# A decoder step on one core: the order in which attention, feed-forward and the samples' work are emitted

## The chip, the cores and the metric

One NeuronCore of a Trainium2 chip runs the whole step in one launch. The metric is the device time of that launch in microseconds (us). The kernel is written with a tile framework: the program emits instructions, and a scheduler at build time places them on the five engine queues (TensorE = PE, VectorE = DVE, ScalarE = ACT, GpSimd = POOL, SyncE = SP, which issues every DMA here). Each queue then runs strictly in the order in which it was written.

## The reference

One layer of a hybrid decoder is run for a prompt (1 sequence of 2048 tokens) and for 8 samples (1 new token each, 1024 tokens of paged past), all in fp32, with D = 1024 and a feed-forward width of 2816.

```python
h = rmsnorm(x) * (1 + sc1) + sh1                      # modulated by c
qkv, z, beta, a, aq, ak, av, iq, ik, iw = split(h @ w_in)
# group 1: gated DeltaNet, 4 heads of 128
#   prompt: chunks of 64; sample: one recurrent step on a 128x128 state per head
s = s * exp(g);  delta = (v - k @ s) * beta;  s = s + outer(k, delta);  o = q @ s
# group 2: sparse attention, 4 heads, 2 kv heads
score = sum_h iw[h] * relu(iq[h] @ ik.T)              # 8 index heads of 64
idx = top_k(score, 256); o_att = softmax(q @ k[idx]) @ v[idx]
x = x + ga1 * (concat(o_gdn, o_att) @ w_out)
x = x + ga2 * ((silu(gate) * up) @ w_ffn_out)         # gate, up = h2 @ w_ffn_in
y = rmsnorm(x)
```

For the prompt the keys of a query are those at or before it, for a sample its 1024 past keys and the new one (1025). New keys, values, convolution rows and recurrent states are outputs too.

## The kernel before, in words

**Precision.** A wide product is done as three fp32r matmuls (`mm3`, lines 157 to 159): both operands are split into a high part and a remainder. `weights` (lines 130 to 146) loads a 128x512 weight tile by DMA (line 140), casts the high part on ACT (line 141) and forms the remainder on DVE (line 142); there are three such tiles (`wi`) and two raw ones (`wr`). For the samples, `mm_s` adds two matmuls per weight tile (lines 173, 174).

**Phase 1** (to about 1430 us) projects the four groups of 512 tokens and runs the DeltaNet chunks; it leaves its results in DRAM. Attention of blocks 0 to 3 (128 queries each) is done there as well.

**Phase 2** has its own pool of buffers. `groups` (lines 1179 to 1190) emits, for g = 0 to 3: the attention of the next four blocks, `ffn(g)`, and after `ffn(0)` the copy of the samples' cache pages (`copy_pages`, 192 copies issued by SP). `sample_steps` is emitted after the attention of blocks 12 to 15 and ahead of `ffn(2)`. What is emitted earlier has the higher priority in the scheduler: where two instructions are ready for an engine, it takes the one emitted first, and a later one fills what is left. An instruction whose buffer is not free can't be placed.

**Attention of a block** is `index` (scores of 8 heads on PE, relu on ACT line 1238, weighted sum on DVE line 1245), then `select` (lines 1119 to 1154), then `attend` (lines 1263 to 1313), which ends with the store of `oT`, of which there is one buffer. `select` looks for the 256th largest score by ten halvings of a threshold: each counts on DVE the scores above it (line 1139) and moves it (lines 1140, 1141); a second part takes out up to 16 keys that are left over. The number of keys still missing is kept in `far`; if any row ever misses more than 16, all of phase 2 is run again with the exact form (`groups(True)`, lines 1174 to 1177).

**`ffn(g)`** multiplies by w_out, adds to x, normalizes, multiplies by w_ffn_in, forms the gated product and multiplies by w_ffn_out. `ffn(3)` carries the 8 samples with it: their output of both head groups (`oTs`) is an operand of its first weight tiles, so its first weight tile is not done before the samples' attention is. Per group it has 192 + 1056 + 528 = 1776 matmuls of `mm3`; `ffn(3)` has 296 of `mm_s` more.

**`sample_steps`** (lines 987 to 1109): the scores of 1025 keys for 8 samples (lines 1027 to 1043), the exact choice of 256 keys by `topk` (32 times line 1116, the 8 largest, and line 1117, which takes them out), then `sample_gdn`, then scores, softmax and values over the whole past with a bias for the keys not chosen (lines 1057 to 1102). It uses attention's buffers: `sc`, `oT`, `PT`, `big`, `qT`, `iqT`, and the PSUM buffers `g` and `s` (two each).

**`sample_gdn`** (lines 881 to 984): the recurrent step. Its small tiles are two `rl` buffers and its large ones the two `big` buffers of attention; the states come in two loads of 1 MB (four samples each).

Of the kernel before, what the change touches and what calls it, by code (L numbers as in the profile page):

```python
# [33 lines left out]
T = 2048  # L34
NS = 8
# [5 lines left out]
H = 4  # L41
# [12 lines left out]
KR = 3  # L54
# [53 lines left out]
class K:  # L108
# [772 lines left out]
    def sample_gdn(self):  # L881
        nc, p, A, O = self.nc, self.p2, self.A, self.O
        raws = self.raws

        def P():
            return self.ps.tile([128, 512], F32, name="g", tag="g", bufs=2)

        def small(*shapes):

            tl, o, views = p.tile([128, 512], F32, name="rl", tag="rl", bufs=2), 0, []  # L890
            for sh in shapes:
                n = int(np.prod(sh))
                v = tl[:, o:o + n]
                views.append(v if len(sh) == 1 else v.rearrange("p (a b) -> p a b", b=sh[1]))
                o += n
            return views

        def big():
            return p.tile([128, T], F32, name="big", tag="big", bufs=2)

        stT, a, b = small((12, 24), (12, NS), (12, NS))
        y, sq, dg, btf, de, o, s2 = small((12, NS), (64,), (64,), (64,), (H, NS), (32,), (32,))
        st, nq = big()[:24, 0:1536], big()[:NS, 0:1536]
        nc.sync.dma_start(st, A["state_conv"][0].rearrange("n i c -> (n i) c"))
        nc.sync.dma_start(O[10][0, :, 0:2, :], A["state_conv"][0, :, 1:3, :])
        pt = P()
        for m in range(12):
            nc.tensor.transpose(pt[:, m * 24:(m + 1) * 24], st[:, m * 128:(m + 1) * 128], self.id[:24, :24])
        nc.vector.tensor_copy(stT, pt[:, :288].rearrange("p (m x) -> p m x", m=12))
        for c in range(3):  # L910
            pt = P()
            for m in range(4):
                nc.tensor.transpose(pt[:NS, m * 128:(m + 1) * 128], raws[:, c * 4 + m, :], self.id)
            nc.vector.tensor_copy(nq[:, c * 512:(c + 1) * 512], pt[:NS])
        nc.sync.dma_start(O[10][0, :, 2, :], nq)
# [28 lines left out]

        for x in range(2):
            S = big().rearrange("p (b h e) -> p b h e", h=H, e=128)
            sl = slice(x * 4, x * 4 + 4)
            nc.sync.dma_start(S, A["state_ssm"][0, sl].rearrange("n h d e -> d n h e"))
            pk = P()
            for s in range(4):  # L950
                for h in range(H):
                    nc.tensor.matmul(pk[:, h * 4 + s:h * 4 + s + 1], S[:, s, h, :], y[:, 4 + h, x * 4 + s:x * 4 + s + 1], start=True, stop=True)
            d = de[:, :, sl]
            nc.vector.tensor_tensor(d, pk[:, :16].rearrange("p (h n) -> p h n", h=H), bt[:, 1, :, sl], op=OP.mult)
            nc.vector.tensor_tensor(d, y[:, 8:12, sl], d, op=OP.subtract)
            nc.vector.tensor_tensor(d, d, bt[:, 0, :, sl], op=OP.mult)
            for s in range(4):
                n = x * 4 + s
                nc.gpsimd.tensor_tensor(S[:, s], S[:, s], bt[:, 1, :, n].unsqueeze(2).to_broadcast([128, H, 128]), op=OP.mult)
                pd = P()  # L960
                for h in range(H):
                    nc.tensor.transpose(pd[:, h * 128:(h + 1) * 128], de[:, h, n:n + 1].to_broadcast([128, 128]), self.id)
                for h in range(H):
                    nc.vector.scalar_tensor_tensor(S[:, s, h, :], pd[:, h * 128:(h + 1) * 128], y[:, 4 + h, n:n + 1], S[:, s, h, :],
                                                   op0=OP.mult, op1=OP.add)
            nc.sync.dma_start(O[11][0, sl].rearrange("n h d e -> d n h e"), S)
            po = P()
            for s in range(4):
                for h in range(H):
                    nc.tensor.matmul(po[:, h * 4 + s:h * 4 + s + 1], S[:, s, h, :], y[:, h, x * 4 + s:x * 4 + s + 1], start=True, stop=True)  # L970
            nc.vector.tensor_copy(o.rearrange("p (h n) -> p h n", h=H)[:, :, sl], po[:, :16].rearrange("p (h n) -> p h n", h=H))
# [7 lines left out]
        gz = big()[:NS, :512]  # L979
# [7 lines left out]
    def sample_steps(self):  # L987
# [16 lines left out]
        b = q.tile([128, T + 16], F32, name="sc", tag="sc", bufs=2)  # L1004
        wk, pr = b[:NS, 0:NK], b[:32, NK:2 * NK]
# [113 lines left out]
    def select(self, pool, w, bias, sums, i):  # L1119


        nc = self.nc
        n = (i + 1) * 128
        s, c = w[:, :n], bias[:, :n]
        v = pool.tile([128, 24], F32, name="sv", tag="sv", bufs=2)
        W = pool.tile([128, SEARCH], F32, name="sW", tag="sW", bufs=2)
# [9 lines left out]
        nc.vector.tensor_scalar(W, self.pw, rg, None, op0=OP.mult)  # L1136
# [8 lines left out]
        nc.vector.scalar_tensor_tensor(self.far[:, 0:1], d, -16.0, self.far[:, 0:1], op0=OP.add, op1=OP.max)  # L1145
        nc.vector.scalar_tensor_tensor(self.far[:, 1:2], d, -1.0, self.far[:, 1:2], op0=OP.mult, op1=OP.max)
        nc.vector.scalar_tensor_tensor(s, c, -(2.0 ** 116), s, op0=OP.mult, op1=OP.add)
        nc.gpsimd.memset(w[:, n:n + 16], PAD)
        for a in range(2):
            nc.vector.max(m8, s)  # L1150
            nc.vector.tensor_scalar(a8, self.io[:, a * 8:a * 8 + 8], d, 3.0e38, op0=OP.is_lt, op1=OP.mult)
            nc.vector.scalar_tensor_tensor(m8, a8, PAD, m8, op0=OP.add, op1=OP.min)
            nc.vector.match_replace(w[:, :n + 16], m8, w[:, :n + 16], GONE)
        nc.vector.tensor_scalar(c, s, -1.0e34, NEG, op0=OP.is_ge, op1=OP.mult)
# [36 lines left out]

    def buffers(self):

        p = self.p2
        one = lambda tag, w, bufs=1, dt=F32: lambda: p.tile([128, w], dt, name=tag, tag=tag, bufs=bufs)
        return dict(pool=p, kT=one("kT", 512, KR), V=one("V", 512, KR), ikT=self.ikT, qT=one("qT", 512), iqT=one("iqT", 1024), sc=one("sc", T + 16, 2),
                    bias=one("bias", T, 2, BF), big=one("big", T, 2), rl=one("rl", 512, 2),
                    PT=one("PT", 512, 2), oT=one("oT", 512, OB))
# [24 lines left out]
    def index(self, i, B, general):  # L1223
        nc, p = self.nc, B["pool"]
        n = (i + 1) * 128
        if i >= 2:
# [24 lines left out]
            else:  # L1251
                self.select(p, sc, bias, None if sums is None else sums[:, :len(self.widths(n))], i)
# [83 lines left out]
    def ffn(self, g):  # L1336
# [27 lines left out]
        if samp:  # L1364
            xrows = q.tile([128, T + 16], F32, name="sc", tag="sc", bufs=2)
# [128 lines left out]
```

## Time and profile before

| | us |
|---|---|
| median of 3 runs | 4013.55 (4011.37 to 4020.09) |
| the profiled execution | 4017.87 |
| its span, first to last instruction | 4016.0 |
| mean granted clock of TensorE | 0.958 of full |
| phase 2, about | 1430 to 4016 |

The profile is one execution. Its views: busy time of each engine over the span and in chosen stretches, groups of like instructions by source line, the instructions in order of time, and the DMA issues. A matmul's length in these views includes its way through the array, so consecutive matmuls overlap; the distance between their starts is what each takes of the engine. `(x2)` and the like count records: an fp32 matmul leaves two.

### The profile page before, as it was taken

The page shows a single profiled execution, that of the slowest core. Times are in us where ns is not written, and L with a number is a line of the kernel's source. Part 1 is how long each engine was busy: PE and PEld are TensorE (multiplying, and loading weights), DVE is VectorE, ACT ScalarE, POOL GpSimd, SP SyncE. Part 2 cuts the span into 40 slices and gives each one's busy share as a digit, 9 for nine tenths or more (in the row PEclk, how much of TensorE's full clock was granted, in tenths as well). Part 3 has the DMA queues.
Part 4 walks back from the last instruction along what each step waited for, and adds up shares of the span by engine and source line. Part 5 has one row for each costly group of instructions (what it writes and reads, how often), then busy time and mean ns, then how long its engine had stood idle before and what let it go on. Part 6 is the DMA issues. An engine that isn't in the chain of part 4 may idle for free.

```text
span 4016.0 us, 50754 instructions
## 1 busy us (share of the span) xinstructions
PE 3688.3 (92%) x17420; PEld 2837.9 (71%) x17420; DVE 2439.4 (61%) x4780; ACT 1365.8 (34%) x2679; POOL 618.4 (15%) x513
## 2 busy tenths in 40 slices
PE   8898988999898899999989999999999977889997
PEld 4777877778676687777767777866877734567775
DVE  3556545554764755877798868599683346144444
ACT  2233324233322433333344343344433331132222
POOL 0000000000000111111130222230211131113223
PEclk9999999999999999999999999999999976999998
DMA  6663454373465324455444323344233332332222
GB/s 238 215 215 129 135 186 146 112 229 126 146 192 196 115 95 146 113 163 157 130 143 132 99 89 103 100 144 130 88 103 105 90 115 95 129 102 79 82 79 70
DMA packets 368309, 528.18 MB, mean 132 GB/s; under 512 B 45612, under 2 KB 246353, under 8 KB 365986
## 3 DMA queue, kind: packets, MB, share of 16 engines
q1 hardware_dynamic: 368042, 524.86, 41.1%
q8 instruction: 139, 2.28, 0.2%
q14 instruction: 128, 1.05, 0.1%
HBM read 427.33 MB, written 116.36 MB: 135 GB/s over the span
## 4 chain that ended last, share of the span: by engine, by line
PE 66%; DVE 16%; DMA 8%; issue 4%; ACT 3%; SPq 2%; POOL 1%; ACTq 0%; DVEq 0%; POOLq 0%
PE d L157 16%; PE d L158 15%; PE d L159 15%; PE g L1304 2%; PE s L1236 2%; DVE wi L142 2%; PE g L800 2%; PE s L1279 1%; PE g L805 1%; DMA wi<-kept 1%; PE g L729 1%; DVE bias L1139 1%; DMA wr<-in_w_ada_dram 1%; PE g L1298 1%; DMA wr<-in_w_ffn_in_dram 1%
## 5 line engine op out<-in xcount | busy, mean ns | idle before, releaser
L142 DVE TENSOR_TENSOR wi<-wr,wi 128x512 fp32r<-128x512 f32 x712 | 530.4, 749 | 696.1 <-ACT wi L141 686.1
L141 ACT CAST wi<-wr 128x512 fp32r<-128x512 f32 x712 | 439.1, 620 | 1088.9 <-PE d L159 425.5
L157 PE MATMUL d<-hh,wi 128*128 128x512 f32 x1792 | 733.7, 410 | 15.6 <-DMA wi<-kept 5.1
L158 PE MATMUL d<-hl,wi 128*128 128x512 f32 x1792 | 715.2, 399 | 0.0
L159 PE MATMUL d<-hh,wi 128*128 128x512 f32 x1792 | 669.2, 402 | 0.0
L157 PEld LDWEIGHTS d<-hh,wi 128*128 128x128 f32 x1792 | 337.8, 189 | 111.2 <-issue 8.6
L1353 POOL TENSOR_TENSOR xt<-xt,tm 128x512 f32<-128x512 f32 x224 | 325.2, 1470 | 527.5 <-DVE tm L1352 424.3
L159 PEld LDWEIGHTS d<-hh,wi 128*128 128x128 f32 x1792 | 336.6, 188 | 88.8 <-issue 8.8
L158 PEld LDWEIGHTS d<-hl,wi 128*128 128x128 f32 x1792 | 338.0, 189 | 78.1 <-issue 6.7
L158 PE MATMUL d<-wi,hh 128*128 128x512 f32 x768 | 311.9, 406 | 3.7 <-DVE wi L142 2.0
L157 PE MATMUL d<-wi,hh 128*128 128x512 f32 x768 | 301.4, 417 | 13.5 <-DMA wi<-kept 10.1
L159 PE MATMUL d<-wi,hl 128*128 128x512 f32 x768 | 307.7, 403 | 0.0
L1425 POOL TENSOR_TENSOR al<-ca,ah 128x512 fp32r<-128x512 f32 x88 | 120.6, 1388 | 1086.4 <-ACT ah L1424 1074.8
L158 PE MATMUL d<-wi,ah 128*128 128x512 f32 x704 | 281.4, 401 | 0.6 <-DVE wi L142 0.5
L157 PE MATMUL d<-wi,ah 128*128 128x512 f32 x704 | 267.6, 415 | 12.1 <-DVE th L1419 4.6
L159 PE MATMUL d<-wi,al 128*128 128x512 f32 x704 | 271.8, 398 | 0.0
L1245 DVE SCALAR_TENSOR_TENSOR sc<-rl,iw,sc 128x512 f32<-128x512 f32 (+3 forms) x224 | 182.1, 813 | 62.6 <-ACT rl L1238 55.2
L1139 DVE TENSOR_SCALAR_CACHE_REDUCE bias<-sc,sv 128x640 bf16<-128x640 f32 (+11 forms) x120 | 193.3, 1610 | 3.0
L1238 ACT ACTIVATE rl<-s 128x512 f32<-128x512 f32 (+3 forms) x288 | 149.8, 543 | 127.4 <-PE s L1236 89.0
L157 PEld LDWEIGHTS d<-wi,hh 128*128 128x128 f32 x768 | 147.6, 194 | 56.6 <-DMA wi<-kept 12.0
L1236 PE MATMUL s<-ik,iqT 128*128 128x512 f32 (+3 forms) x576 | 162.6, 387 | 18.5 <-ACT rl L1238 16.1
L1352 DVE TENSOR_TENSOR tm<-d,row 128x512 f32<-128x512 f32 x224 | 149.4, 681 | 48.3 <-PE d L159 31.2
(504 smaller groups left out, 5917.0 us busy)
## 6 DMA issues: line engine op xcount, KB each, us to landing
wr<-in_w_ffn_in_dram SPq DMA_DIRECT2D x704, 128.0 KB, 2.2
wi<-kept SPq DMA_DIRECT2D x168, 512.0 KB, 3.4
wr<-in_w_ffn_out_dram SPq DMA_DIRECT2D x176, 256.0 KB, 2.6
kept<-wi SPq DMA_DIRECT2D x56, 512.0 KB, 3.5
xt<-in_x_prompt_dram SPq DMA_DIRECT2D x8, 2048.0 KB, 8.2
wr<-in_w_ada_dram SPq DMA_DIRECT2D x64, 256.0 KB, 2.8
wr<-in_w_out_dram SPq DMA_DIRECT2D x64, 256.0 KB, 2.6
wr<-in_w_in_dram SPq DMA_DIRECT2D x56, 256.0 KB, 3.8
```

The costliest lines, as they stand in the source:

```text
L141: nc.scalar.copy(w[:, 0], wr)
L142: nc.vector.tensor_tensor(w[:, 1], wr, w[:, 0].bitcast(F32), op=OP.subtract)
L157: nc.tensor.matmul(out, wh, xh, start=start, stop=False, **kw)
L158: nc.tensor.matmul(out, wh, xl, start=False, stop=False, **kw)
L159: nc.tensor.matmul(out, wl, xh, start=False, stop=stop, **kw)
L1139: nc.vector.tensor_scalar(c, s, t, None, op0=OP.is_ge, op1=OP.add, accum_out=cnt)
L1236: nc.tensor.matmul(ps[:, :w], iq[:, h, :].bitcast(F32R), B["ikT"][c * 2 + a][:, :w].bitcast(F32R), start=a == 0, stop=a == 1)
L1238: nc.scalar.activation(r[:, :w], ps[:, :w], AF.Relu)
L1245: nc.vector.scalar_tensor_tensor(s, r[:, :w], iw, s, op0=OP.mult, op1=OP.add)
L1352: nc.vector.tensor_tensor(tm[:rows], pd[:rows], rw, op=OP.mult)
L1353: nc.gpsimd.tensor_tensor(xt, xt, tm[:rows], op=OP.add)
L1425: nc.gpsimd.tensor_tensor(al[b], a, ah[b].bitcast(F32), op=OP.subtract)
```

## The change

`sample_gdn` gets its own tiles: one of 128x832 for the small values (`gs`) and two of 128x512 (`gS`) for what was in `big`. Its large pieces are cut to that size: the convolution rows in three parts, the states one sample at a time (8 loads and 8 stores of 256 KB instead of 2 and 2 of 1 MB). The number of matmuls and transposes stays; the three small DVE steps per batch of four become three per sample, and the copy of the output as well. It is no longer called inside `sample_steps` but after `ffn(0)` and `copy_pages`.

`select` takes the number of keys and of rows, and a separate output; `sample_steps` calls it for the 8 rows of 1025 scores in place of `topk` and of line 1045. The samples' rows now count in `far` as well, and the exact form is used for them in `groups(True)`.

`groups` is written out: attention of blocks 8 to 11 is emitted ahead of `ffn(0)`, that of blocks 12 to 15 ahead of `ffn(1)`, and `sample_steps` stays ahead of `ffn(2)`.

```diff
     def sample_gdn(self):
+        tl, at = p.tile([128, 832], F32, name="gs", bufs=1), [0]
...
-        def small(*shapes):
-            tl, o, views = p.tile([128, 512], F32, name="rl", tag="rl", bufs=2), 0, []
...
         def big():
-            return p.tile([128, T], F32, name="big", tag="big", bufs=2)
+            return p.tile([128, 512], F32, name="gS", tag="gS", bufs=2)
...
-        for x in range(2):
-            S = big().rearrange("p (b h e) -> p b h e", h=H, e=128)
-            sl = slice(x * 4, x * 4 + 4)
-            nc.sync.dma_start(S, A["state_ssm"][0, sl].rearrange("n h d e -> d n h e"))
+        for n in range(NS):
+            S = big().rearrange("p (h e) -> p h e", h=H)
+            nc.sync.dma_start(S, A["state_ssm"][0, n].rearrange("h d e -> d h e"))
             pk = P()
-            for s in range(4):
-                for h in range(H):
-                    nc.tensor.matmul(pk[:, h * 4 + s:h * 4 + s + 1], S[:, s, h, :], ...)
+            for h in range(H):
+                nc.tensor.matmul(pk[:, h:h + 1], S[:, h, :], y[:, 4 + h, n:n + 1], start=True, stop=True)
+            d = de[:, :, n]
+            nc.vector.tensor_tensor(d, pk[:, :H], bt[:, 1, :, n], op=OP.mult)
+            nc.vector.tensor_tensor(d, y[:, 8:12, n], d, op=OP.subtract)
+            nc.vector.tensor_tensor(d, d, bt[:, 0, :, n], op=OP.mult)
+            nc.gpsimd.tensor_tensor(S, S, bt[:, 1, :, n].unsqueeze(2).to_broadcast([128, H, 128]), op=OP.mult)
+            pd = P()
+            for h in range(H):
+                nc.tensor.transpose(pd[:, h * 128:(h + 1) * 128], de[:, h, n:n + 1].to_broadcast([128, 128]), self.id)
+            for h in range(H):
+                nc.vector.scalar_tensor_tensor(S[:, h, :], pd[:, h * 128:(h + 1) * 128], y[:, 4 + h, n:n + 1], S[:, h, :],
+                                               op0=OP.mult, op1=OP.add)
+            nc.sync.dma_start(O[11][0, n].rearrange("h d e -> d h e"), S)
             po = P()
+            for h in range(H):
+                nc.tensor.matmul(po[:, h:h + 1], S[:, h, :], y[:, h, n:n + 1], start=True, stop=True)
+            nc.vector.tensor_copy(ov[:, :, n], po[:, :H])
...
-    def sample_steps(self):
+    def sample_steps(self, general):
...
-        self.topk(q, wk, NS)
-        nc.vector.tensor_scalar(wk, wk, -2.0e38, NEG, op0=OP.is_ge, op1=OP.mult)
-        self.sample_gdn()
+        if general:
+            self.topk(q, wk, NS)
+            nc.vector.tensor_scalar(wk, wk, -2.0e38, NEG, op0=OP.is_ge, op1=OP.mult)
+        else:
+            self.select(q, b0[:NS], q.tile([128, T], BF, name="bias", tag="bias", bufs=2)[:NS, :NK], None, NK, NS, wk)
...
-    def select(self, pool, w, bias, sums, i):
+    def select(self, pool, w, c, sums, n, rows=128, out=None):
...
-        nc.vector.tensor_tensor(s[:, n - 128:n], s[:, n - 128:n], self.caus, op=OP.add)
+        if out is None:
+            nc.vector.tensor_tensor(s[:, n - 128:n], s[:, n - 128:n], self.caus, op=OP.add)
...
     def groups(self, general):
...
-        for g in range(self.ng):
-            if g + 1 < self.ng:
-                self.attn(range(g * 4 + 4, g * 4 + 8), B, general, g * 4 + 8 if g + 2 < self.ng else None)
-            if g == self.ng - 2 and not general:
-                self.sample_steps()
-            self.ffn(g)
-            if g == 0 and not general:
-                self.copy_pages()
+        self.attn(range(4, 8), B, general, 8)
+        self.attn(range(8, 12), B, general, 12)
+        self.ffn(0)
+        if not general:
+            self.copy_pages()
+            self.sample_gdn()
+        self.attn(range(12, 16), B, general)
+        self.ffn(1)
+        self.sample_steps(general)
+        self.ffn(2)
+        self.ffn(3)
```

## Rows read from the trace of the kernel before

**Rows 1.** The page, part 1: busy time of each engine.

```profile
PE 3688.3 (92%) x17420; PEld 2837.9 (71%) x17420; DVE 2439.4 (61%) x4780; ACT 1365.8 (34%) x2679; POOL 618.4 (15%) x513
```

**Rows 2.** Busy time by stage: us, then each engine's, PEclk, DMA share, GB/s.

```profile
1430.00:1700.00 270.00, 258.71 (x1295) 211.20 (x1295) 183.11 (x373) 97.82 (x186) 48.52 (x42) 0.99 0.39 117
1700.00:2000.00 300.00, 286.07 (x1237) 224.15 (x1236) 222.92 (x455) 111.29 (x209) 52.20 (x39) 0.98 0.52 152
2000.00:2200.00 200.00, 181.46 (x774) 136.21 (x773) 181.47 (x343) 88.71 (x176) 44.93 (x33) 0.97 0.43 139
2200.00:2600.00 400.00, 397.54 (x1755) 315.74 (x1754) 289.06 (x479) 158.16 (x281) 87.75 (x59) 1.00 0.32 95
2600.00:2800.00 200.00, 183.14 (x795) 135.98 (x794) 183.14 (x325) 90.42 (x170) 42.49 (x33) 0.99 0.43 140
2800.00:3248.00 448.00, 445.34 (x1947) 335.73 (x1945) 251.68 (x423) 166.83 (x280) 105.23 (x93) 1.00 0.33 100
3248.00:3476.00 228.00, 171.03 (x632) 87.47 (x632) 104.02 (x185) 35.23 (x72) 29.26 (x41) 0.71 0.33 114
3476.00:4016.00 540.00, 491.06 (x2112) 368.72 (x2110) 238.96 (x350) 154.72 (x294) 132.87 (x108) 0.96 0.27 83
...
3276.00:3362.00 86.00, 46.99 (x186) 34.59 (x184) 76.31 (x137) 2.23 (x5) 18.89 (x9) 0.50 0.18 53
```

**Rows 3.** First and last start of three lines, from the view of one line.

```profile
L1313 SPq DMA_DIRECT2D oT_d<-oT x12: 359/377/420, 1706.6 to 3187.6; - x12
...
L1029 SPq DMA_DIRECT2D PT<-ikp_d x8: 320/375/786, 3186.0 to 3263.4; - x8
...
L1108 DVE COPY oTs<-g x2: 184/184/184, 3473.1 to 3473.6; 128x16 f32<-128x16 f32 x2
```

**Rows 4.** Costliest groups between 3248 and 3476: busy us, mean ns, idle before.

```profile
L1116 DVE MAX8 m<-sc 8x8 f32<-8x1025 f32 x32 | 38.8, 1213 | 0.5
...
L952 PE MATMUL g<-rl,big 128*128 128x1 f32 x64 | 13.9, 352 | 13.1 <-DVE rl L932 13.1
...
L190 POOL TENSOR_TENSOR rnsz<-rnsy,mhalf 128x64 f32<-128x64 f32 x1 | 10.5, 10518 | 48.8 <-DVE rnsy L188 48.8
...
L962 PE MATMUL g<-cf,rl 128*128 128x128 f32 x32 | 8.2, 429 | 10.3 <-DVE rl L956 7.1 <-DVE big L964 3.2
```

**Rows 5.** TensorE in order of time near 3208: start us, length us, instruction.

```profile
3207.75 1.02 PE L1041 MATMUL s<-big,oT 8*8 8x512 f32 x2
3208.70 0.63 PE L1035 MATMUL g<-cf,PT 128*64 128x128 f32 x4
3209.08 0.48 PE L159 MATMUL d<-hh,wi 128*128 128x512 f32 x1
3209.40 0.39 PE L157 MATMUL d<-hh,wi 128*128 128x512 f32 x1
3209.63 0.39 PE L158 MATMUL d<-hl,wi 128*128 128x512 f32 x1
```

**Rows 6.** TensorE in order of time near 3397.

```profile
3397.15 0.66 PE L1064 MATMUL g<-cf,big 128*128 128x128 f32 x4
3397.74 1.04 PE L1067 MATMUL s<-PT,qT 128*32 128x512 f32 x2
3398.71 0.66 PE L1064 MATMUL g<-cf,big 128*128 128x128 f32 x4
```

**Rows 7.** TensorE in order of time near 3456.

```profile
3456.07 7.11 PE L1101 MATMUL s<-big,iqT 128*32 128x256 f32 x32 [1.48 <-DMA big<-vp_d]
```

**Rows 8.** Groups of the search's lines on VectorE, shapes apart.

```profile
L1141 DVE SCALAR_TENSOR_TENSOR sv<-sv,sW 128x1 f32<-128x1 f32 x140 | 38.4, 275 | 2.7
...
L1139 DVE TENSOR_SCALAR_CACHE_REDUCE bias<-sc,sv 128x1024 bf16<-128x1024 f32 x10 | 12.8, 1278 | 0.3
```

**Rows 9.** DMA issues: 256 KB (page, part 6); 1 MB (landing of line 948).

```profile
wr<-in_w_ffn_out_dram SPq DMA_DIRECT2D x176, 256.0 KB, 2.6
...
DMA to landing us min/median/max: 6.5/6.5/6.5
```

More of the change, by code (lines that the diff above doesn't have):

```diff
@@ L883, in sample_gdn, with small @@
         raws = self.raws
+        tl, at = p.tile([128, 832], F32, name="gs", bufs=1), [0]
         def P():
             return self.ps.tile([128, 512], F32, name="g", tag="g", bufs=2)
-        def small(*shapes):
-            tl, o, views = p.tile([128, 512], F32, name="rl", tag="rl", bufs=2), 0, []
[L891 to L896, printed above, removed]
-        def big():
-            return p.tile([128, T], F32, name="big", tag="big", bufs=2)
[L901 to L904, printed above, removed]
+        def small(*sh):
+            n = int(np.prod(sh))
+            v = tl[:, at[0]:at[0] + n]
+            at[0] += n
+            return v if len(sh) == 1 else v.rearrange("p (a b) -> p a b", b=sh[1])
+        def big():
+            return p.tile([128, 512], F32, name="gS", tag="gS", bufs=2)
+        stT, a, b = small(12, 24), small(12, NS), small(12, NS)
+        y, sq, dg, btf, de, o = small(12, NS), small(64), small(64), small(64), small(H, NS), small(32)
         nc.sync.dma_start(O[10][0, :, 0:2, :], A["state_conv"][0, :, 1:3, :])
[L906 to L909, printed above, removed]
         for c in range(3):
+            cs = slice(c * 512, (c + 1) * 512)
+            st = big()[:24]
+            nc.sync.dma_start(st, A["state_conv"][0].rearrange("n i c -> (n i) c")[:, cs])
+            pt = P()
+            for m in range(4):
+                nc.tensor.transpose(pt[:, m * 24:(m + 1) * 24], st[:, m * 128:(m + 1) * 128], self.id[:24, :24])
+            nc.vector.tensor_copy(stT[:, c * 4:c * 4 + 4, :], pt[:, :96].rearrange("p (m x) -> p m x", m=4))
             pt = P()
@@ L913, in sample_gdn @@
                 nc.tensor.transpose(pt[:NS, m * 128:(m + 1) * 128], raws[:, c * 4 + m, :], self.id)
-            nc.vector.tensor_copy(nq[:, c * 512:(c + 1) * 512], pt[:NS])
-        nc.sync.dma_start(O[10][0, :, 2, :], nq)
+            nq = big()[:NS]
+            nc.vector.tensor_copy(nq, pt[:NS])
+            nc.sync.dma_start(O[10][0, :, 2, cs], nq)
         w = lambda i: self.cv[:, 64 + i * 12:76 + i * 12].unsqueeze(2).to_broadcast([128, 12, NS])
@@ L949, in sample_gdn @@
             pk = P()
-            for s in range(4):
-                for h in range(H):
[L952 to L965, printed above, removed]
@@ L967, in sample_gdn @@
+            pd = P()
[5 more added lines that the diff above has]
+            nc.sync.dma_start(O[11][0, n].rearrange("h d e -> d h e"), S)
             po = P()
-            for s in range(4):
-                for h in range(H):
-                    nc.tensor.matmul(po[:, h * 4 + s:h * 4 + s + 1], S[:, s, h, :], y[:, h, x * 4 + s:x * 4 + s + 1], start=True, stop=True)
@@ L978, in sample_gdn @@
         pz = P()
-        gz = big()[:NS, :512]
+        gz = big()[:NS]
         nc.sync.dma_start(gz, self.gzs_d)
@@ L1002, in mid @@
             return q.tile([128, 512], F32, name="PT", tag="PT", bufs=2)
-        b = q.tile([128, T + 16], F32, name="sc", tag="sc", bufs=2)
-        wk, pr = b[:NS, 0:NK], b[:32, NK:2 * NK]
+        b0 = q.tile([128, T + 18], F32, name="sc", tag="sc", bufs=2)
+        wk, pr = b0[:NS, 0:NK], b0[:32, NK + 16:2 * NK + 16]
         b = q.tile([128, 512], F32, name="oT", tag="oT", bufs=OB)
@@ L1117, in topk @@
             nc.vector.match_replace(wk, m8[:rows], wk, GONE)
-    def select(self, pool, w, bias, sums, i):
+    def select(self, pool, w, c, sums, n, rows=128, out=None):
         nc = self.nc
[L1123 to L1126, printed above, removed]
+        s, io, pw, far = w[:, :n], self.io[:rows], self.pw[:rows], self.far[:rows]
+        v = pool.tile([128, 24], F32, name="sv", tag="sv", bufs=2)[:rows]
+        W = pool.tile([128, SEARCH], F32, name="sW", tag="sW", bufs=2)[:rows]
         m8, lo, rg, t, d, cnt, a8 = v[:, 0:8], v[:, 8:9], v[:, 9:10], v[:, 10:11], v[:, 11:12], v[:, 12:13], v[:, 16:24]
@@ L1144, in select @@
         nc.vector.tensor_scalar(d, cnt, -1.0, float(TOPK), op0=OP.mult, op1=OP.add)
-        nc.vector.scalar_tensor_tensor(self.far[:, 0:1], d, -16.0, self.far[:, 0:1], op0=OP.add, op1=OP.max)
-        nc.vector.scalar_tensor_tensor(self.far[:, 1:2], d, -1.0, self.far[:, 1:2], op0=OP.mult, op1=OP.max)
+        nc.vector.scalar_tensor_tensor(far[:, 0:1], d, -16.0, far[:, 0:1], op0=OP.add, op1=OP.max)
+        nc.vector.scalar_tensor_tensor(far[:, 1:2], d, -1.0, far[:, 1:2], op0=OP.mult, op1=OP.max)
         nc.vector.scalar_tensor_tensor(s, c, -(2.0 ** 116), s, op0=OP.mult, op1=OP.add)
@@ L1150, in select @@
             nc.vector.max(m8, s)
-            nc.vector.tensor_scalar(a8, self.io[:, a * 8:a * 8 + 8], d, 3.0e38, op0=OP.is_lt, op1=OP.mult)
+            nc.vector.tensor_scalar(a8, io[:, a * 8:a * 8 + 8], d, 3.0e38, op0=OP.is_lt, op1=OP.mult)
             nc.vector.scalar_tensor_tensor(m8, a8, PAD, m8, op0=OP.add, op1=OP.min)
             nc.vector.match_replace(w[:, :n + 16], m8, w[:, :n + 16], GONE)
-        nc.vector.tensor_scalar(c, s, -1.0e34, NEG, op0=OP.is_ge, op1=OP.mult)
+        nc.vector.tensor_scalar(c if out is None else out, s, -1.0e34, NEG, op0=OP.is_ge, op1=OP.mult)
     def phase2(self, es):
@@ L1195, in buffers @@
         one = lambda tag, w, bufs=1, dt=F32: lambda: p.tile([128, w], dt, name=tag, tag=tag, bufs=bufs)
-        return dict(pool=p, kT=one("kT", 512, KR), V=one("V", 512, KR), ikT=self.ikT, qT=one("qT", 512), iqT=one("iqT", 1024), sc=one("sc", T + 16, 2),
+        return dict(pool=p, kT=one("kT", 512, KR), V=one("V", 512, KR), ikT=self.ikT, qT=one("qT", 512), iqT=one("iqT", 1024), sc=one("sc", T + 18, 2),
                     bias=one("bias", T, 2, BF), big=one("big", T, 2), rl=one("rl", 512, 2),
@@ L1251, in index @@
             else:
-                self.select(p, sc, bias, None if sums is None else sums[:, :len(self.widths(n))], i)
+                self.select(p, sc, bias[:, :n], None if sums is None else sums[:, :len(self.widths(n))], n)
         else:
@@ L1364, in ffn @@
         if samp:
-            xrows = q.tile([128, T + 16], F32, name="sc", tag="sc", bufs=2)
+            xrows = q.tile([128, T + 18], F32, name="sc", tag="sc", bufs=2)
             xs, rws = xrows[:NS, 0:D], xrows[:NS, D:2 * D]
```

6 lines of the change are left out of this document (3 added, 3 removed).

## The prediction

> **What bounds the kernel now.** I read the page first: TensorE is busy for 92% of the span, VectorE for 61% [rows 1]. So the sum goes by TensorE's work, and the question is where that engine stands still. The view by stages answers it [rows 2]. From 1430 to 3248 us, where attention runs beside `ffn(0)` to `ffn(2)`, TensorE is idle for 11.3 + 13.9 + 18.5 + 2.5 + 16.9 + 2.8 = 66 of 1818 us. From 3248 to 3476 it is busy for 171 of 228 us, at a mean granted clock of 0.71, and between 3276 and 3362, where it is busy for 47 of 86 us, the clock is 0.50, its lower level of 1.2 GHz. From 3476 on the samples' rows ride in `ffn(3)`: 540 us.
>
> What fills 3248 to 3476 is the samples alone. The view of single lines shows why it lies there [rows 3]: the first load of `sample_steps` (line 1029) starts at 3186.0, next to the last store of attention's `oT` (line 1313) at 3187.6; the tile that `sample_steps` takes is the one `oT` buffer. Its last instruction, line 1108, comes at 3473.6. By then `ffn(2)` is through and `ffn(3)` can't go past its first weight tiles without `oTs`. So 228 us of latency stand nearly bare at the end of a kernel that is otherwise limited by TensorE.
>
> **The change, part by part.**
>
> *The order.* With attention of blocks 8 to 11 ahead of `ffn(0)` and of 12 to 15 ahead of `ffn(1)`, attention shares TensorE with two groups instead of three. When does it end? TensorE was busy for 258.7 + 286.1 + 181.5 + 397.5 + 183.1 + 445.3 = 1752 us from 1430 to 3248 [rows 2]. `ffn(2)` is 1776 matmuls at 0.233 us each (the starts 3209.40 and 3209.63 [rows 5]), 414 us; about 20 us are samples' scores. That leaves 1318 us for attention, `ffn(0)` and `ffn(1)`; with some 50 of the 66 idle us they end near 1430 + 1368 = 2798, and `sample_steps` can begin then. It then has the 414 us of `ffn(2)` and its own TensorE work as cover. At its present pace it needs 3474 - 3186 = 288 us, of which the part that leaves it (next paragraphs) is over 60. So the samples are done some 200 us before `ffn(3)` asks for them.
>
> What goes is therefore the idle part of the 228 us; the TensorE work in it stays and must be priced at full clock and back to back. Distances between starts give that. Lines 1039 and 1041 take 3208.70 - 3207.75 = 0.95 us for two records; four of line 1035 take 0.38 [rows 5]. After 3248 there are 16 + 16 + 24 records: 7.6 + 7.6 + 2.3 us. Four transposes of line 1064 with two records of line 1067 take 3398.71 - 3397.15 = 1.56 us, 32 times [rows 6]: 50 us. Line 1101 takes 7.1 us for 32 records, four times [rows 7]: 28.4 us. The recurrent step's lines 952 and 970 (a second group like the first) are 13.9 us each and line 962 8.2 us, all at the half clock [rows 2, 4]: 36 us there, 18 us at the full one. Some 5 us are small ones. Sum: 119 us. In the same stretch 42 matmuls of `ffn(3)` were done, 10 us. So 228 - 119 - 10 = 99 us go.
>
> Two other readings of the same rows bound this term. By busy time only 228 - 171 = 57 us would go. By weight loads, busy for 335.7 of 448 us in the dense stretch before and for 87.5 here, the stretch holds 87.5 / 0.75 = 117 us of dense work, and 111 go [rows 2]. I take 99, since it counts each instruction.
>
> The Trainium skill (Trainium Kernel Development and Optimization, Performance Expectations) bears on the choice: it calls matmul busy time a bad measure, since matmuls are pipelined, and names the share of weight loads instead. By it the sum would be 12 us lower than mine, by busy time 42 higher; the distances between starts agree with the page.
>
> *What the fuller stages cost.* Where attention had priority over `ffn(1)`, from 2200 to 2600, TensorE lost 0.6% [rows 2]; the losses lie where page copies run (1700 to 2000) and where one group hands over to the next with VectorE at 91% (2000 to 2200 and 2600 to 2800). The first two stay. The handover to `ffn(2)` may have attention finished and may lose less; that to `ffn(3)` has nothing left to fill it. Bounds: 8 us better (half of 16.9), and 56 worse, if all of 1540 to 2750 falls to the 9.3% of 2000 to 2200 (112 us against about 56 now). I take 5 us worse, nearest to the sum of the rows as they are.
>
> *The recurrent step early.* The same matmuls are in the 119 us. VectorE gets 18 small steps more (24 for 6) and 6 copies of the output more: with the 0.28 us of the search's one-column step [rows 8] as their length, 7 us, hidden by TensorE, which VectorE trails by 30% in these stages; uncovered it costs 7. SP gets 12 more state transfers and 4 more of the convolution rows, at 0.38 us of issue (line 1313 [rows 3]) 6 us, beside the weight loads. Behind a store that waits on SP stand these loads; three split tiles of 12 matmuls cover 12 x 3 x 0.233 = 8.4 us. POOL has a power of 10.5 us [rows 4] ahead of the adds to x; behind it waits at most one add, for which the four `d` buffers of PSUM wait. I cost it at nothing, with 0 to 30 us as bounds if all three are bare; nothing gained either, because this work has to be done somewhere.
>
> The Trainium skill (DMA: Bandwidth & Descriptors, Measured) has a rule against this split: batch transfers to 1 MB or more. The rows say that a 1 MB state load lands after 6.5 us and a 256 KB transfer after 2.6 [rows 9], so eight take 21 us for 13; neither reaches the end as long as `ffn` matmuls lie beside it. On the page's figure of about 2 us fixed per transfer, 12 more would be an estimated 24 us if each stood bare, and the sum 3944.
>
> *The search.* `topk` is 32 pairs of 1.21 us [rows 4] (line 1117 is as long), 78 us of VectorE. Ten halvings at 1.28 + 0.28 us, plus a middle step that I take as no longer than 0.28, are 18 us [rows 8]; the count, the minimum, the maximum and the removal are about nine more passes of 1.28: 12 us. So 30 for 78. It shortens the samples' chain by 48 us, which has cover by then: worth 0 on the end here, and up to 48 if the chain is still bare. In a bare chain the recurrent step lay within the `topk`.
>
> **The sum**, against the profiled execution's own time of 4017.87 us (span 4016.0): 4017.9 - 99 + 5 = 3924. The median of the runs lies 4.3 us lower, 0.1%; so 4013.6 - 94 = 3920 us.
>
> **Rivals.**
>
> *The samples stay late.* If attention fills in as before and ends near 3190, the `oT` buffer holds `sample_steps` back, and only the recurrent step and 48 us of search leave the bare stretch. Between 3276 and 3362, 86 us, the 30 us of search would be left: 56 us gained, 3958. For it: the start at 3186 next to the last `oT` [rows 3]. Against it: priority over `ffn(1)` in 2200 to 2600 went with full progress.
>
> *VectorE saturates.* The state of 2000 to 2200 (VectorE and TensorE both at 91%) over all of attention: 99 - 56 = 43 us gained, 3971. Against it: VectorE's work is the same, over two thirds of the time: 290 us of 400 in 2200 to 2600 leaves room.
>
> *TensorE stands in the recurrent step (slower).* Each queue runs in its written order. For each sample TensorE waits for a load, for three chained VectorE steps and for four updates. If the scheduler thinks them quick and puts nothing between, each of about five visits to VectorE stands behind one or two of attention's passes of 1.3 to 2.6 us (1.28 at width 1024 [rows 8]; width 2048 taken as double). That is some 16 us a sample, 128 us, and 16 for the powers: 3920 + 144 = 4064. It decides from 94 / 8 = 12 us a sample. For it: the bare step now hops between four engines. Against it: other multi-hop chains (attention itself) stand among `ffn` matmuls with 0.6% lost.
>
> *It is run again.* If a sample's search left over 16 keys, all of phase 2 would be repeated: 2586 us more, about 6500. Worked out from the reference's inputs, the search leaves 1, 2, 2, 2, 0, 0, 1 and 0 keys for the eight samples. Under 1 in 100.
>
> *More.* Handover losses shrink as well and the weight-load reading holds: 111 + 8 gained, 3895 and a little below.
>
> **How the numbers follow.** The forecast with its own range of 3895 to 3948: 0.60. Samples late 0.13; VectorE saturated 0.11; more (below 3895) 0.08; TensorE standing or run again 0.05; no change, by half of that standing, 0.03. Cases of the forecast and the rivals on the same side reach from 119 us gained to 43. With a little beyond each end the range is 3878 to 3978; below it lie 0.05 and above it 0.11. A change of under 0.2% (8 us) can't be told from none here: faster 0.92, within it 0.03, slower 0.05.
>
> **What would show it.** The stretch with a clock near 0.5 late in phase 2 is gone; line 1029 starts before 2900, and line 1108 ends over 100 us ahead of the first w_out matmul of `ffn(3)`; line 948 starts near 1600 to 2200; 11 counting passes of 1.28 us stand in place of lines 1116 and 1117; `ffn(3)` still takes 540 us. I am wrong on the first step if line 1029 starts after 3100; on the price of the fuller stages if TensorE's share from 1540 to 2750 is below 0.92; on the recurrent step if TensorE's waits at lines 952 to 970 are above 30 us together.

## The result, and the profile after

The changed kernel takes 3964.5 us (median of 4 runs, 3954.5 to 3970.8) against 4016.8 for the kernel before in the same runs: a ratio of 0.9869, 95% interval 0.9844 to 0.9894. That is faster by 52 us; 3920 was predicted, and 3964 lies inside the range. But the trace shows another way to it than the likeliest case had. Of the experiments below, one execution of e9 (12506.5 us) and one of e10 (9890.5 us) fell far outside the others and is left out of the ratios; why they did is open.

The page of the profiled execution after (span 3969.0 us), part 1, which answers to [rows 1]:

```profile
PE 3680.2 (93%) x17420; PEld 2828.2 (71%) x17420; DVE 2387.7 (60%) x4772; ACT 1367.1 (34%) x2679; POOL 615.6 (16%) x514
```

Busy time by stage after, columns as in [rows 2]; the stretch 3239 to 3428 answers to the bare one of before, 3248 to 3476:

```profile
1700.00:2000.00 300.00, 283.58 (x1224) 220.89 (x1223) 223.96 (x455) 111.37 (x209) 52.25 (x39) 0.98 0.52 150
2000.00:2200.00 200.00, 182.78 (x782) 138.31 (x781) 176.68 (x344) 91.97 (x180) 42.35 (x32) 0.95 0.44 141
2200.00:2600.00 400.00, 399.61 (x1797) 316.18 (x1796) 308.40 (x568) 156.84 (x278) 93.42 (x60) 1.00 0.33 99
2600.00:2800.00 200.00, 180.12 (x833) 143.02 (x832) 133.57 (x245) 78.06 (x153) 57.20 (x41) 0.94 0.45 142
2800.00:3239.00 439.00, 434.84 (x1907) 340.45 (x1906) 280.71 (x476) 158.06 (x258) 85.97 (x77) 1.00 0.32 95
3239.00:3428.00 189.00, 175.28 (x614) 67.67 (x613) 56.33 (x113) 56.50 (x109) 29.29 (x48) 0.85 0.42 145
3428.00:3969.00 541.00, 492.00 (x2114) 368.61 (x2112) 240.15 (x350) 155.46 (x295) 131.91 (x108) 0.96 0.27 83
...
1540.00:2750.00 1210.00, 1147.66 (x5073) 897.64 (x5072) 928.72 (x1821) 470.07 (x880) 277.11 (x202) 0.98 0.43 128
```

Three lines after, each from the view of one line, which answer to [rows 3]: attention's stores of `oT`, the samples' first loads (now line 1024), their last copy (now line 1105).

```profile
L1313 SPq DMA_DIRECT2D oT_d<-oT x12: 359/378/1065, 1711.1 to 3240.8; - x12
...
L1024 SPq DMA_DIRECT2D PT<-ikp_d x8: 319/326/528, 3239.7 to 3302.5; - x8
...
L1105 DVE COPY oTs<-g x2: 184/186/188, 3425.7 to 3426.2; 128x16 f32<-128x16 f32 x2
```

Attention does not end earlier. Its last store moved from 3188 to 3241, 53 us later, and `sample_steps` still starts beside that store, 1.1 us ahead of it. What got shorter is the samples' chain itself: 3239.7 to 3426.2 is 187 us against 288, because the recurrent step has left it and the search is short. 101 us less of chain, 54 us of later start: 47 us net at the point where `ffn(3)` can go on, of 52 in the time. `ffn(3)` takes 541 us, 540 before.

Where attention's time goes shows in its instructions on TensorE in order of time, after, while block 11 is attended (start us, length us; of the matmuls of `ffn(1)`, which fill every gap, only the first is shown), and behind it ACT's copy of the first transposes, from the same view of ACT:

```profile
2439.19 1.03 PE L1304 MATMUL g<-PT,V 128*128 128x256 f32 x4
2440.05 0.60 PE L1298 MATMUL g<-cf,big 128*128 128x128 f32 x4
2440.41 0.48 PE L158 MATMUL d<-hl,wi 128*128 128x512 f32 x1
...
2445.16 1.02 PE L1304 MATMUL g<-PT,V 128*128 128x256 f32 x4
2446.02 0.60 PE L1298 MATMUL g<-cf,big 128*128 128x128 f32 x4
...
2452.06 1.02 PE L1304 MATMUL g<-PT,V 128*128 128x256 f32 x4
2452.92 0.60 PE L1298 MATMUL g<-cf,big 128*128 128x128 f32 x4
...
2458.03 1.02 PE L1304 MATMUL g<-PT,V 128*128 128x256 f32 x4
...
2440.69 0.59 ACT L1301 COPY PT<-g 128x512 f32<-128x512 f32 x1 [1.52 <-PE g L1298]
```

Four transposes (line 1298) go into a PSUM buffer, ACT copies them out, two value matmuls (line 1304, two records each) use the copy. The two together take about 1.2 us of TensorE (2439.19 to 2440.41), yet a step takes 6.0 to 6.9 us: the other 4.7 us and more are feed-forward matmuls that stand in the queue between one visit of attention and the next. The copy is over at 2441.28, so the value matmuls of 2445.16 have their operand, and the bank is free, 3.9 us before they start: they stand behind matmuls that were written ahead of them at build time. TensorE is busy for 399.6 of 400 us from 2200 to 2600, so no busy share shows that attention is waiting.

From this came two theories. **A**, the prediction's: what is emitted first gets TensorE first, so attention's end goes by how much TensorE work is emitted ahead of it. **B**: attention is a chain of some 350 visits to TensorE in series, 144 for the index, 72 for scores, 132 for steps like those above, counted from the program (the expectations below have 126 steps and 340 visits); after each, its next instruction can't be placed until a PSUM buffer is free by the scheduler's reckoning (two `s`, two `g`, of which the attended sum holds one), and by then some 20 feed-forward matmuls stand ahead of it (4.7 us at 0.233 [rows 5]). B says that the pace is set by the buffers, and the order of emission matters little.

### The profile page after: what moved, and what is told of

Read it like the earlier page. It is cut to its first block, busy times and chain, and to the rows that moved or that the text cites. A ratio compares the mean times of both kernels' runs of the same rounds, so it can differ in the third digit from the quotient of the medians.

```text
span 3969.0 us, 50790 instructions
## 1 busy us (share of the span) xinstructions
PE 3680.2 (93%) x17420; PEld 2828.2 (71%) x17420; DVE 2387.7 (60%) x4772; ACT 1367.1 (34%) x2679; POOL 615.6 (16%) x514
## 5 line engine op out<-in xcount | busy, mean ns | idle before, releaser
L1136 DVE TENSOR_SCALAR_CACHE_REDUCE bias<-sc,sv 128x640 bf16<-128x640 f32 (+12 forms) x130 | 206.0, 1585 | 3.0
L157 PEld LDWEIGHTS d<-wi,ah 128*128 128x128 f32 x704 | 133.6, 191 | 67.3 <-ACT ah L1424 7.8
```

Source lines behind the costliest of these rows:

```text
L157: nc.tensor.matmul(out, wh, xh, start=start, stop=False, **kw)
```

## The experiments

Ratios are to the kernel before, run on the same chip, with 95% intervals. From set to set its median was 4007 to 4017 us, so differences of times between rows are rough: through the ratios e2, e3 and e7 are 41, 41 and 30 us slower than the kernel after, where the times give 37, 36 and 24, each give or take 11 to 13.

| | time, us | ratio | last `oT` store | samples' last copy |
|---|---|---|---|---|
| before | 4016.8 | 1 | 3188 | 3474 |
| after | 3964.5 | 0.9869 [0.9844, 0.9894] | 3241 | 3426 |
| e1 order alone | 3982.2 | 0.9932 [0.9913, 0.9950] | 3126 | 3434 |
| e2 old order | 4001.8 | 0.9970 [0.9959, 0.9980] | 3275 | 3457 |
| e3 recurrent late | 4000.2 | 0.9971 [0.9958, 0.9984] | 3135 | 3455 |
| e4 attention first | 3974.4 | 0.9905 [0.9888, 0.9921] | 3132 | 3431 |
| e5 four banks, after | 3942.9 | 0.9829 [0.9809, 0.9849] | 3013 | 3317 |
| e6 four banks, before | 3935.1 | 0.9814 [0.9792, 0.9835] | 2979 | 3387 |
| e7 old selection | 3988.9 | 0.9944 [0.9924, 0.9964] | 3231 | 3441 |
| e8 fewer steps | 3860.2 | 0.9616 [0.9590, 0.9641] | 2906 | 3207 |
| e9 e5 + recurrent late | 3937.5 | 0.9828 [0.9813, 0.9843] | 2862 | 3321 |
| e10 e9 + old order | 3937.6 | 0.9825 [0.9809, 0.9840] | 2980 | 3390 |

**e1: the order alone**, on the kernel before.

```diff
+        self.attn(range(4, 8), B, general, 8)
+        self.attn(range(8, 12), B, general, 12)
+        self.ffn(0)
+        if not general:
+            self.copy_pages()
+        self.attn(range(12, 16), B, general)
+        self.ffn(1)
+        if not general:
+            self.sample_steps()
+        self.ffn(2)
+        self.ffn(3)
```

> The kernel before with the new order of emission alone (recurrent step and exact top-k where they were). Theory A, order (the prediction's): attention emitted a group ahead runs a group ahead and ends near 2800, so line 1029 starts before 2900 and about 90 of the 94 us are won: 3925. Theory B, returns: attention comes back to TensorE about 340 times, and each time its instructions stand behind some 16 to 20 feed-forward matmuls already queued (about 5 us), so its end is set by the number of returns and hardly by the order: attention ends between 3100 and 3250, time 3960 to 4000.

Attention ends at 3126: 61 us earlier than before, where A asks for nearly 400. B's numbers hold.

**e2: the change with the old order**, the recurrent step after `copy_pages`.

```diff
-        self.attn(range(4, 8), B, general, 8)
-        self.attn(range(8, 12), B, general, 12)
...
+        for g in range(self.ng):
+            if g + 1 < self.ng:
+                self.attn(range(g * 4 + 4, g * 4 + 8), B, general, ...)
+            if g == self.ng - 2:
+                self.sample_steps(general)
+            self.ffn(g)
+            if g == 0 and not general:
+                self.copy_pages()
+                self.sample_gdn()
```

> The changed kernel with the old order of emission; the early recurrent step and the search stay. Theory A: without the order the samples stay late, and only the recurrent step and the search are won: 3958 to 3985, clearly slower than the changed kernel. Theory B: the same range, but next to the changed kernel (3964), within 25 us, since the order did little there.

Both miss. The order is worth 37 us of time on top of the rest: more than the 25 that B allowed, far less than the 90 that A gave it in e1.

**e3: the recurrent step late**, in its own buffers but inside `sample_steps`, after the search.

```diff
             self.copy_pages()
-            self.sample_gdn()
...
             self.select(q, b0[:NS], ..., NK, NS, wk)
+            self.sample_gdn()
```

> The changed kernel with the recurrent step (in its own buffers) back inside sample_steps, after the search. Theory A: the step was hidden for nothing where it is now, so putting it back costs what it takes bare beside the search, 40 to 60 us: 4005 to 4025. Theory B: the early step's own returns through the two g buffers of PSUM held attention up by about 60 us; without them attention ends near 3180, which gives back most of that: 3945 to 3975.

Neither. Attention ends 106 us earlier without the step in its way (3135 for 3241), and the kernel is still 36 us slower, since the step now stands in the bare chain. So the early step delays attention by about 100 us and pays all the same. e3 is also 18 us slower than e1, whose selection is the long one. There the step's matmuls (3269 to 3325) lie inside the `topk` (3243 to 3355); in e3 the search is over at 3305 and the step's matmuls, 3298 to 3353, come behind it. So a short search uncovers the step, and its gain and the step's price can't be subtracted from one another. What the cut into eight loads costs is open: it was not run alone.

**e4: all attention emitted ahead of all feed-forward.**

```diff
         self.attn(range(8, 12), B, general, 12)
+        self.attn(range(12, 16), B, general)
         self.ffn(0)
...
-        self.attn(range(12, 16), B, general)
         self.ffn(1)
```

> The changed kernel with all attention (blocks 4 to 15) emitted ahead of every feed-forward group. Theory A: attention ends before 2600, the samples are done within ffn(1) or early in ffn(2): 3920 or less. Theory B: the number of returns is the same, so the last oT store stays between 3180 and 3270 and the time within 25 us of 3964.

3132: with all of attention first, it ends where e1 has it. A falls here: the order was pushed to its limit and attention still ran from 1430 to 3132. B has the time right and the end 48 us too late, since here the recurrent step is emitted behind attention.

**e5 and e6: free banks.** The tags `g` and `s` of PSUM, two banks each, become one tag of four; the same edit in the kernel after (e5) and in the kernel before (e6), at each place where one of the two is taken.

```diff
-            po = self.ps.tile([128, 512], F32, name="g", tag="g", bufs=2)
+            po = self.ps.tile([128, 512], F32, name="s", tag="s", bufs=4)
...
-                    ps = self.ps.tile([128, 512], F32, name="s", tag="s", bufs=2)
+                    ps = self.ps.tile([128, 512], F32, name="s", tag="s", bufs=4)
```

> The kernel after, with one edit: the two PSUM tags g and s, two banks each, become one tag of four banks; so scores, index products, transposes, attend's sum and the samples' products may take whichever of the four is free. No instruction is added or left out. Theory B (attention comes back to TensorE some 340 times in series, and each return stands behind 16 to 20 feed-forward matmuls already queued, about 5 us; the number of returns is set by the banks that are free): with up to four banks for one stream a return carries more work, so there are fewer. The last oT store moves from 3241 to 2850-2950 us, the samples' products with the keys (line 1024) begin below 2960, the samples end before the feed-forward of group 3 begins, the stretch 3200-3500 shows no TensorE share below 95, and the time is 3860-3925 us. Theory A (the order of emission is the order of running, and the delay of attention has another cause than the banks): last oT store within 40 us of 3241, time within 15 us of 3964.

> The kernel before, with the same single edit (one tag of four PSUM banks in place of two tags of two). Theory B: the banks act without any part of the change: last oT store from 3188 to 2850-2950 us, the samples' chain (288 us long in the kernel before) begins there and is over or nearly so when the feed-forward of group 3 begins; time 3900-3960 us, and the rest of the change is then worth 0-50 us on top of it. Theory A: last oT store within 40 us of 3188, time within 15 us of 4013.

No instruction is added, and attention ends 228 us earlier in e5 and 209 in e6, 63 and 29 us short of B's bounds. B's time is missed by 18 us in e5 and holds in e6; A, with no change, is far off in both. Both beat the changed kernel, and e6, the kernel before with nothing but this edit, gains 79 us where the whole change gained 52. The stores of `oT` in e5 and in e6, and the samples' last copy in e6, from the view of one line:

```profile
L1313 SPq DMA_DIRECT2D oT_d<-oT x12: 360/420/468, 1706.8 to 3013.3; - x12
...
L1313 SPq DMA_DIRECT2D oT_d<-oT x12: 359/406/983, 1702.9 to 2978.8; - x12
...
L1108 DVE COPY oTs<-s x2: 184/184/185, 3386.5 to 3387.0; 128x16 f32<-128x16 f32 x2
```

The samples' whole chain now lies beside `ffn(2)`: in e6, from 2979 to 3387, TensorE is busy for 402.5 of 408 us.

```profile
2979.00:3387.00 408.00, 402.52 (x1721) 264.02 (x1720) 201.32 (x335) 116.18 (x210) 106.69 (x95) 0.97 0.38 123
3390.00:3930.00 540.00, 490.08 (x2109) 368.60 (x2107) 236.86 (x349) 154.60 (x293) 132.31 (x108) 0.96 0.27 85
```

How the banks do it was not as B put it. The same view as above, of e5 while block 11 is attended (lines 1298 and 1304 alone):

```profile
2324.73 1.05 PE L1304 MATMUL s<-PT,V 128*128 128x256 f32 x4
...
2325.61 1.47 PE L1298 MATMUL s<-cf,big 128*128 128x128 f32 x12
...
2328.78 1.03 PE L1304 MATMUL s<-PT,V 128*128 128x256 f32 x4
2329.64 0.60 PE L1298 MATMUL s<-cf,big 128*128 128x128 f32 x4
2330.08 1.03 PE L1304 MATMUL s<-PT,V 128*128 128x256 f32 x4
```

Three steps' transposes go in one visit here, and the value matmuls follow at 4.1 and 1.3 us instead of 6 to 7. But over block 11 as a whole (counted from the same view between two stores of `oT`) the visits are not fewer: 40 in e5 over 118 us, 35 in the kernel after over 154. They come closer: 3.0 us apart in the mean for 4.4. The reading that fits is that with a bank free attention has a next instruction to place while the last one is still being copied out. That the banks set the pace is shown by e5 and e6; what the scheduler took the copies to last, which also decides how many matmuls it writes in between, is not in a trace and was not tested.

**e7: the old selection for the samples.**

```diff
-        if general:
+        if True:
             self.topk(q, wk, NS)
```

> The kernel after, with the samples' keys found again by rounds of eight maxima (lines 1116 and 1117 of the kernel before) in place of the threshold search of 11 counting passes. Samples' selection in the kernel before: 3348 to about 3400, in bare time. Both theories put the samples' chain at 3241 to 3428 here, most of it bare, so the price of the selection is seen whole: 20 to 45 us slower than the kernel after (3984-4010). If the selection is hidden beside the feed-forward, as the prediction's likeliest case had it: within 8 us of 3964.

24 us slower than the kernel after: the search was bare, not covered. The search itself, after, VectorE's groups between 3300 and 3360 (lines 1136 and 1140 are the eleven counting passes):

```profile
L1136 DVE TENSOR_SCALAR_CACHE_REDUCE bias<-sc,sv 8x1025 bf16<-8x1025 f32 x10 | 12.7, 1272 | 0.4
L1150 DVE MATCH_REPLACE8 sc<-sv,sc 8x1041 f32<-8x1041 f32 x2 | 2.4, 1216 | 0.0
L1147 DVE MAX8 sv<-sc 8x8 f32<-8x1025 f32 x2 | 2.4, 1210 | 0.0
L1138 DVE SCALAR_TENSOR_TENSOR sv<-sv,sW 8x1 f32<-8x1 f32 x10 | 2.1, 207 | 0.4
...
L1140 DVE TENSOR_SCALAR_CACHE_REDUCE bias<-sc,sv 8x1025 bf16<-8x1025 f32 x1 | 1.3, 1272 | 0.0
```

**e8: fewer steps.** Probabilities are transposed and multiplied by the values for the first four key blocks only.

```diff
-            for b0 in range(0, i + 1, 2):
+            for b0 in range(0, min(i + 1, 4), 2):
```

> The kernel after, which leaves out the probabilities' transposes and their products with the values for all key blocks of a query block but the first four (that part of attention is not computed). It takes away 60 of the 126 steps of two transposed key blocks; banks and order are as in the kernel after. Own TensorE work of a step, transposes and products, is about 1.2 us (estimate: a step of 6.0 us at 2440-2458 less 4.5 to 5 us of feed-forward matmuls), so about 70 us of work goes. Theory A: the last oT store comes 70 us earlier at most, 3170-3241, and the time is 3890-3935. Theory B: each step that goes takes its return of 5 to 6 us with it: last oT store 2880-2960, samples done within the feed-forward of group 2, time 3770-3860.

The expectation counts the steps wrongly. Each has one copy on ACT (line 1301), and the views of that line, after and in e8, show 132 and 48, so 84 steps go:

```profile
L1301 ACT COPY PT<-g x132: 366/587/599, 1664.6 to 3233.7; 128x512 f32<-128x512 f32 x120, 128x256 f32<-128x256 f32 x12
...
L1301 ACT COPY PT<-g x48: 565/587/597, 1658.2 to 2901.6; 128x512 f32<-128x512 f32 x48
```

Their own work is some 95 us (72 at 1.2 us, 12 of half the size), and the last store comes 334 us earlier: 4.0 us for each step, more than three times what it takes of TensorE. That is far beyond A, which allows the work alone. It is less than B's 5 to 6 us, which for 84 steps ask for 2737 to 2821, and near the 4.4 us between visits over the whole of block 11. The time, at the upper edge of what B expected, tells little: of its 104 us about 95 are work left out.

**e9 and e10: is anything of the change left once the banks are free?** e9 is e5 with e3's move; e10 has the old order of emission as well.

```diff
-            self.sample_gdn()
         self.attn(range(12, 16), B, general)
...
+            self.sample_gdn()
```

> The kernel after with one tag of four PSUM banks (as e5) and the samples' recurrent step emitted inside the samples' chain after its search (as e3). In e3 against the kernel after the late step brought the attention's end forward by 106 us and lost 36 us of time, because the chain was bare there. Theory B with free banks: the last oT store comes near 2910 (3013 less about 100), the whole samples' chain of some 290 us lies inside the feed-forward of group 2, which ends near 3400, so the place of the recurrent step is worth nothing: 3930-3948, within 10 us of e5 (3943). Rival (the early step is worth its 36 us wherever the chain lies): 3970-3985.

> As e9, and with the old order of emission too (attention one group ahead of the feed-forward): what is left of the change is the samples' search and the recurrent step's own buffers. Theory B with free banks: attention ends near 2980 as in e6, the samples' chain lies inside the feed-forward of group 2, the order is worth nothing: 3928-3948, within 10 us of e6 (3935) and of e9. Rival (the new order is worth the 37 us that e2 showed, whatever the banks): 30 us or more above e9.

B's times hold in both; in e9 attention ends 48 us earlier than expected, and the covered chain takes 459 us, not 290. Attention's end spreads from 2862 (e9) to 3013 (e5), and the four kernels with free banks lie within 8 us: 3935.1, 3937.5, 3937.6, 3942.9, with overlapping intervals. Moving the recurrent step, the order and the search, worth 36, 37 and 24 us where the chain is bare, are worth nothing that can be measured where it is covered. The stores of `oT` in e9:

```profile
L1313 SPq DMA_DIRECT2D oT_d<-oT x12: 359/430/469, 1713.1 to 2862.3; - x12
```

For attention's end itself both still count, and more than with two banks: the early step holds it up by 151 us (3013 in e5, 2862 in e9; 106 with two), and the order brings it forward by 118 (2980 in e10, 2862 in e9; 61 with two, e1). So B's second half, that the order matters little, holds for the time only.

## Why the range held and the mechanism did not

**What bounds the kernel**: right. The bare samples' chain was the place to gain; e6 covers it whole and gains 79 us.

**The order**: the step that failed. The sum was: TensorE's idle 50 us aside, attention, `ffn(0)` and `ffn(1)` are 1318 us, and "they end near 1430 + 1368 = 2798". Measured: 3241 after, and 3126 with the order alone. The step took a busy TensorE for a TensorE that works by priority. A priority counts only when the instruction can be placed; attention's next one was written some 20 feed-forward matmuls behind the last after each visit, and more banks alone brought its end forward by 209 and 228 us (e5, e6). My own evidence for it, 0.6% lost from 2200 to 2600, told how well TensorE was filled, not by whom. The sign set down beforehand, "I am wrong on the first step if line 1029 starts after 3100", is what came: 3240 (now line 1024).

**The rival "samples stay late"** is the case that came: attention's buffers hold `sample_steps` back, and the recurrent step and the search alone leave the bare stretch. (The first load goes into `PT`, 1.1 us ahead of the last store of `oT`, so it did not wait for `oT`; which of the buffers binds was not tested.) It gave 3958; 3964.5 was measured. It had been given 0.13, so that the time fell inside the range is owed to this rival and not to the sum, which gave 94 us for the 52 measured: as far as the forecast goes, luck. It left the order out, which e2 shows to carry 37 us of the 52, and the early step's delay of attention, which took much of that back.

**The 99 us for covered samples**: oversized. e6 has all of it covered and gains 79. Of the readings weighed, busy time said 57, distances between starts 99 and weight loads 111. The Trainium skill (Trainium Kernel Development and Optimization, Performance Expectations) names the share of weight loads, beside the share of peak arithmetic, as the measure of how near a kernel is to its limit; as a price for this stretch it was too high, and the measurement lies between the first two. Why 20 us of the 99 were not there is open.

**Fuller stages**: right in size. TensorE is busy for 1147.7 of 1210 us from 1540 to 2750, a share of 0.948 and above the 0.92 named as the sign; 62 us idle against the 56 estimated for before. But attention still ran beside `ffn(2)`, so the stages were hardly fuller than before, and the price was not put to the test.

**The recurrent step early**: costed at nothing, and so it is for TensorE, which did not stand for it. Its waits between 2500 and 2700, after, at the step's own lines are 1.5 us (the sign was 30):

```profile
PE g L957 <- DVE gs L953: 0.9, 1, 0.9
PE g L964 <- DVE gS L959: 0.6, 1, 0.6
```

What the sum lacked is who else waits. The step's matmuls run from 2561 to 2667, emitted ahead of blocks 12 to 15 and in the `g` banks that attention uses as well; behind them the last matmul of attention before the step's end and the next one, in order of time:

```profile
L949 PE MATMUL g<-gs,gS x64: 165/250/250, 2561.6 to 2659.1; 128*128 128x1 f32 x64
L964 PE MATMUL g<-gs,gS x64: 164/250/290, 2578.2 to 2667.4; 128*128 128x1 f32 x64
...
2587.25 1.02 PE L1279 MATMUL s<-kT,qT 128*128 128x512 f32 x2
...
2681.52 0.60 PE L1298 MATMUL g<-cf,big 128*128 128x128 f32 x4
```

For 94 us attention has no matmul on TensorE at all; in e3, with the step late, no such gap is longer than 7 us. Those in the `s` banks ran on until 2587, and the first to come back is one in `g`. In e5, with one tag for both, all of attention stands from 2381 to 2506, 125 us. Both fit banks that are given out in the order of emission, the step's before block 12's; that was not tested by itself. Block 12's store comes 247 us after block 11's; with the step late (e3) it is 172. In all, attention's end moved by 106 us. I had asked which engine would stand, and not which chain.

**The search**: eleven counting passes of 1.27 us are there, and all of it takes 30 us (3329 to 3359), as predicted. "Worth 0 on the end here, and up to 48 if the chain is still bare": it was bare, and e7 gives 24. A selection in a bare chain does not stop everything else: in e7 the samples' last copy comes 47 us after the selection, in the kernel after 67.

**The slower rivals** did not come. VectorE did not saturate (308 of 400 us from 2200 to 2600).

## What to carry to other kernels

On an engine that is always busy, ask whose work fills it: take one chain, look at its consecutive instructions there and divide each step into its own time and what stands between. If a high-priority chain gives the engine back after every step, moving it earlier in the program gained less here (61 us of its end) than buffers that let its next instruction be queued before the last is done (209), and gained more once they were there (118). What is emitted ahead of such a chain and shares its buffers can stop it altogether, though the engine stays busy. And a latency chain that is covered is worth nothing to shorten: find the cover first (here one tag of four banks, 79 us), then see what is left for the rest.

## What was unexpected

A full TensorE hid a lack of PSUM. The Trainium skill (Perfetto Trace Analysis, Identifying Performance Opportunities) takes a gap that repeats on the engine that should be saturated as a possible sign that SBUF or PSUM ran out. Here there was no gap to see, 399.6 of 400 us busy, and the two banks of a tag still held attention's end back by more than 200 us (e5, e6): the sign lay in the distances within one chain.

The same one-column matmul of the recurrent step shows the clock. In e3, where the step is bare, it is 0.352 us long at a granted clock of 0.50 from 3298 to 3349, the lower level; in the kernel after, beside `ffn(1)`, it is 0.250 in the median at a mean of 0.92 from 2561 to 2668. In e3 TensorE was busy for 34.6 of the 51 us, in the kernel after for 97.5 of 107. The view of line 949 in e3, and both stretches:

```profile
L949 PE MATMUL g<-gs,gS x64: 352/352/371, 3298.2 to 3348.2; 128*128 128x1 f32 x64
```

```profile
3298.00:3349.00 51.00, 34.64 (x148) 31.26 (x148) 23.76 (x74) 0.00 (x0) 7.64 (x8) 0.50 0.35 108
...
2561.00:2668.00 107.00, 97.49 (x464) 77.74 (x463) 91.49 (x192) 29.63 (x50) 46.58 (x36) 0.92 0.42 122
```
